# A hybrid encoder layer on one core: the low half of a split weight on VectorE or GpSimd

## The chip, the core and the metric

The kernel runs on one core of a Trainium2 chip. The metric is the device time of one execution in microseconds. The core has TensorE (matmul, "PE" in the profile, its weight loads "PEld"), VectorE ("DVE"), ScalarE ("ACT"), GpSimd ("POOL") and SyncE ("SP", here only the issuer of DMAs). Each engine works through its own stream of instructions in the order in which the program was written, and waits for others at semaphores.

## What is computed

One encoder layer over 512 tokens of 1024 features in float32: two token mixers in parallel, merged by gates, then a SwiGLU channel mixer.

```python
proj = h @ w_in[l]
qa, ka, va, qb, kb, vb = jnp.split(proj, SPLITS, axis=-1)
...
o_a = windowed_gqa_sink(qa, ka, va, a_sink[l])
o_b = dilated_mixture(qb, kb, vb)
gates = jax.nn.sigmoid(h @ w_gate[l] + b_gate[l])
g_a, g_b = jnp.split(gates, N_BRANCH, axis=-1)
mixed = g_a * (o_a @ w_br_a[l]) + g_b * (o_b @ w_br_b[l])
y = mixed @ w_out[l]
h = layer_norm(DN_ALPHA * h + y, ln1_g[l], ln1_b[l])
f = (jax.nn.silu(h @ w_ff_gate[l]) * (h @ w_ff_up[l])) @ w_ff_down[l]
h = layer_norm(DN_ALPHA * h + f, ln2_g[l], ln2_b[l])
```

Mixer A is windowed attention with 16 query heads and 4 key heads and a sink; mixer B is three dilated windows of attention, combined by their softmax denominators.

## The kernel before

**Split operands.** A float32 operand `w` is turned into `hi`, the value rounded to the format that TensorE takes at full pace, and `lo = w - hi`. Every product is then three matmuls: `hi*hi`, `hi*lo`, `lo*hi` (lines 456 to 458 in the projections and branches, 650 to 652 in mixer B's values, 1077 to 1079 in the output projection and the end of the channel mixer, 1312 to 1314 and 1441 to 1443 in the channel mixer). The weights come from HBM packed as `wpack` in units of 128x1024; a half unit is a tile of 128x512. `half_unit` (line 359) loads a half unit into a tile of class `ws`, takes two tiles of class `whl` for `hi` and `lo`, and calls `split` (line 350): first a copy that makes `hi`, by ScalarE or VectorE (`copy`, line 333 for ScalarE and 335 for VectorE), then the subtraction that makes `lo`, line 354, by VectorE. `unit` calls it twice, `token_values` (mixer B's values) calls `split` itself. The very first weights (line 382), the input (line 430), the attention's own operands (lines 528, 544, 563, 683, 702), the branches' moving operands (`split_of`, line 998) and the channel mixer's weights (`parts`, line 1199, by ScalarE and VectorE) have code of their own. So 130 subtractions come from line 354: 122 for `w_in`, the gates, the branches and `w_out`, 8 for the last rows of `w_ff_down`.

**Stages,** by the time in the trace: start of the projections (to 20 us), projections with mixer A between them (20 to about 230), with mixer B (240 to 345), the two branches and the gates' products (345 to about 390), output projection and first layer norm (to 446), channel mixer (446 to 740), its last rows, second layer norm and store (740 to 780). Attention is laid between the dense matmuls: for a unit of mixer A (a group of heads and 128 queries) scores (lines 578 and 579), a maximum and mask on VectorE (726), the exponential on ScalarE (730), a scaling by either (666, 668), four transposes on TensorE (678), a split by ScalarE and VectorE (333, 683), the product with the values (743, 744). A unit of mixer B has the same parts (786 to 818, 678 and 693, 870 and 904) and in its middle an exchange of statistics between partitions, 32 small copies on GpSimd (lines 828 and 829).

**The order.** No order is written out for the engines. Each operation is handed to `op` with a list of engines that may do it and a cost for each; `Program.run` (line 171) then plays the program forward with these costs, and whenever an engine is free it takes the ready operation with the lowest `prio`, and emits it. A copy has two possible engines. VectorE passes over an operation with more than one engine as long as ScalarE is free or is about to be:

```python
if o.ready <= now and (best is None or o.prio < best.prio) and self.fits(o):
    if e == DVE and len(o.alts) > 1 and free[ACT] < now + BIAS:
        continue
    best = o
```

`prio` is the time on TensorE's plan at which the operation was written down, plus an offset: -130 (`LOOK`) for weights, so that they are made early, -100 for what empties PSUM, 0 for attention's inner steps, -20 for the splits of line 998. `fits` holds an operation back while there are no free tiles of its class: 16 tiles `whl` until the last attention unit has ended, 40 then.

**GpSimd before** does 16 DMAs of the rotary tables (line 435), 64 copies of the sink (724) and four pairs of memsets (767, 768) for the attention units, 128 copies of mixer B's exchange (828, 829), 80 DMAs that add a second matrix to a weight tile on its way (1266), and four additions in the second layer norm (1129), ahead of which it is set up once for such arithmetic.

Of the kernel before, what the change touches and what calls it, by code (L numbers as in the profile page):

```python
# [13 lines left out]
ALU = mybir.AluOpType  # L14

P = 128
S = 512
# [28 lines left out]
PE, ACT, DVE, POOL, SP = "PE", "ACT", "DVE", "POOL", "SP"  # L46
# [6 lines left out]
N_BEGIN = 2  # L53
N_HALF = 3
N_LAST1, N_LAST, BY_POOL = 5, 4, (1, 2)
BANKS = dict(dense=3, s=2, tb=2, o=1, d=8)
UNITS = 2
D_BANK = "s"
# [39 lines left out]
class Program:  # L98
# [16 lines left out]
    def op(self, alts, fn, reads=(), writes=(), prio=0.0, after=(), abs_prio=None, moves=0.0):  # L115
        o = Op()
        o.urgent = self.urgent
        o.alts, o.fn = alts, fn
        o.prio = (self.T + prio if abs_prio is None else abs_prio, len(self.ops))
        o.ready, o.done, o.eng = 0.0, None, None  # L120
        deps = set(a for a in after if a is not None)
        for t in reads:
            deps.update(self.writer.get(t, ()))
        for t in writes:
            deps.update(self.writer.get(t, ()))
            deps.update(self.readers.get(t, ()))
        deps.discard(o)
        for t in reads:
            self.readers.setdefault(t, []).append(o)
        for t in writes:  # L130
            self.writer[t] = [o]
            self.readers[t] = []
        o.bufs, o.new = [], []
        o.strict, o.moves = self.strict, moves
        for t in list(reads) + list(writes):
            b = self.buf_of(t)
            if b not in o.bufs:
                o.bufs.append(b)
                b.users += 1
        o.succ = []  # L140
        o.left = len(deps)
        for d in deps:
            d.succ.append(o)
        self.ops.append(o)
        return o
# [134 lines left out]
def dve(n, fast=False, extra=0.0):  # L280
    return 0.069 + (0.00074 if fast else 0.00104) * n + extra
# [7 lines left out]
def hybrid_layer(ctx: ExitStack, tc: tile.TileContext, wpack, xT, xtok, sink, bgate,  # L289
                 ln1g, ln1b, ln2g, ln2b, ropec, ropes, maska, maskb, identd, out):  # L290
    nc = tc.nc
# [5 lines left out]
    N_SLOT = 85 - 2 * N_TWO  # L297
    pr = Program({"slot": N_SLOT, "bank": 8, **BANKS,
                  "ws": N_WS, "whl": N_WHL, "att": N_ATT, "gen": N_SLOT - 2 - N_ATT - N_WS - N_WHL,
                  "unit": UNITS, "st": 4, "x4": 4, "wf": N_WF, "two": N_TWO})  # L300
    op = pr.op
# [29 lines left out]
    def copy(eng, dst, src):  # L331
        if eng == ACT:
            nc.scalar.activation(dst, src, AF.Copy)  # L333
        else:
            nc.vector.tensor_copy(dst, src)

    def f32(ap):
        return ap.bitcast(F32)
# [5 lines left out]
    def cp_alts(n, ps=False):  # L344
        return [(ACT, act(n, ps)), (DVE, dve(n, not ps))]
# [4 lines left out]
    def split(src, h, l, prio=0.0, abs_prio=None, hold=()):  # L350

        op(cp_alts(S), lambda e: copy(e, h.t, src.t), reads=[src], writes=[h, *hold], prio=prio,
           abs_prio=abs_prio)
        op([(DVE, dve(S))], lambda e: nc.vector.tensor_tensor(l.t, src.t, f32(h.t), op=ALU.subtract),  # L354
           reads=[src, h], writes=[l], prio=prio, abs_prio=abs_prio)

    LOOK, LOOK_E, LOOK_W, LOOK_U, LOOK_T = 130.0, 80.0, 30.0, 15.0, (-300.0, -118.0, -114.5, -108.0)

    def half_unit(u, j, look=LOOK):
        st, h, l = slot(F32, "ws"), slot(F32R, "whl"), slot(F32R, "whl")  # L360
        load(st, wpack[u, :, j * S:(j + 1) * S], prio=-look)
        split(st, h, l, prio=-look, hold=[(l, "room")])
        return h, l
# [69 lines left out]
    for t_, src, ap in ((cosT, ropec, -119.5), (sinT, ropes, -119.4)):  # L433
        for i in range(8):
            op([(POOL, 1.0)], lambda e, t_=t_, i=i, src=src: nc.gpsimd.dma_start(t_.t[16 * i:16 * i + 16], src[0:16]),
               writes=[(t_, i)], abs_prio=ap, moves=0.1)
# [5 lines left out]
       reads=[nsink], writes=[nsink], abs_prio=-119)  # L442
# [189 lines left out]
    def token_values():  # L632

        parts_ = []
        for k in range(KD):
            st, h, l = slot(F32, "ws"), slot(F32R, "whl"), slot(F32R, "whl")
            u, c = U_VB + k // 4, (k % 4) * 256
            load(st, wpack[u:u + 3:2, :, c:c + 256].rearrange("g p c -> p g c"),
                 dst=lambda st=st: st.t.rearrange("p (g c) -> p g c", g=2), prio=-LOOK)
            split(st, h, l, prio=-LOOK, hold=[(l, "room")])  # L640
            parts_.append((h, l))
        res = ([], [])
        for r in range(NR):
            ps = bank("dense")
            for k in range(KD):
                wh, wl = parts_[k]

                def go(e, ps=ps, k=k, wh=wh, wl=wl, r=r):
                    a, b = xh[k]()[:, r * P:(r + 1) * P], xl[k]()[:, r * P:(r + 1) * P]
                    mm(ps.t, a, wh.t, start=(k == 0), stop=False)  # L650
                    mm(ps.t, a, wl.t, start=False, stop=False)
                    mm(ps.t, b, wh.t, start=False, stop=(k == KD - 1))

                op([(PE, 3 * pe(S))], go, reads=[wh, wl, *xtok_of(k)], writes=[ps])
                pr.T += 3 * pe(S)
            for g in range(2):
                res[g].append(value_split(ps, 256 * g))
        return res
# [350 lines left out]
    for f in range(16):  # L1009
        op([(ACT, act(S))], lambda e, f=f: nc.scalar.activation(gz[f].t, gz[f].t, AF.Sigmoid),  # L1010
           reads=[gz[f]], writes=[gz[f]], after=exps)
# [588 lines left out]
```

## Time and profile before

| | us |
|---|---|
| median of three runs | 781.47 (781.02 to 781.51) |
| the profiled execution's own time | 781.53 |
| its span, first to last instruction | 779.8 |
| ScalarE's copies, line 333, from SBUF and from PSUM, busy | 242.5 and 88.6 |
| line 354 on VectorE, busy | 87.0 |
| the exchange on GpSimd, lines 828 and 829, busy | 16.7 and 16.8 |

The page is one execution. Its groups read: line, engine, operation, output from inputs (`sl` a tile of the slab, `ps` a PSUM bank, `tw`, `x` other tiles, `st` statistics), count, busy time and mean of one, then how long the engine was idle before them and for whom. Stage rows read: the stretch, its length, then busy time and count of PE, PEld, DVE, ACT and POOL, the granted clock of TensorE, the DMA engines' share and GB/s. A timeline row is start, length, engine, line and operation. Work outside the span takes 781.53 - 779.8 = 1.7 us.

### The profile page before, as it was taken

How to read it: one execution, taken by the hardware profiler on the slowest of the kernel's cores; microseconds unless marked ns; L12 is line 12 of the kernel's file. 1: busy time of each engine (PE TensorE's matmuls, PEld its weight loads, DVE VectorE, ACT ScalarE, POOL GpSimd, SP SyncE). 2: the span in 40 equal slices, each digit the busy share in tenths (PEclk: the TensorE clock that was granted, in tenths of full speed). 3: DMA queues.
4: the chain of work that ended last, by engine and by line, in shares of the span. 5: the costliest groups of instructions: out<-in, count | busy, mean ns of one | idle time of the engine just before them, and what ended most of it. 6: DMA issues, size and time to landing. Idle time of an engine off the chain costs nothing.

```text
span 779.8 us, 13408 instructions
## 1 busy us (share of the span) xinstructions
PE 769.9 (99%) x4486; PEld 676.6 (87%) x4486; DVE 652.5 (84%) x1377; ACT 480.9 (62%) x1061; POOL 131.5 (17%) x304
## 2 busy tenths in 40 slices
PE   9999999999999999999999999999999999999996
PEld 5888888888888888888888899999999999999985
DVE  5689889898778999797687999887988889888697
ACT  5557787868757668794341667566655566555631
POOL 4100001100000801600011010242102331123002
PEclk9999999999999999999999999999999999999999
DMA  8642323213132324436373388689867987689102
GB/s 268 217 138 71 99 88 105 83 44 108 57 96 88 104 87 145 142 111 201 121 217 67 109 231 225 155 183 213 227 179 161 241 179 208 182 213 210 52 1 108
DMA packets 64901, 111.79 MB, mean 143 GB/s; under 512 B 8640, under 2 KB 12352, under 8 KB 64832
## 3 DMA queue, kind: packets, MB, share of 16 engines
q1 hardware_dynamic: 52656, 89.37, 35.5%
q0 software_dynamic: 12032, 21.50, 16.5%
q8 instruction: 35, 0.57, 0.3%
q14 instruction: 34, 0.28, 0.1%
q10 hardware_dynamic: 144, 0.07, 0.0%
HBM read 104.09 MB, written 3.93 MB: 139 GB/s over the span
## 4 chain that ended last, share of the span: by engine, by line
PE 93%; DVE 2%; ACT 1%; DMA 1%; issue 1%; SPq 1%; DVEq 0%
PE ps L457 11%; PE ps L456 11%; PE ps L458 11%; PE ps L1314 9%; PE ps L1313 9%; PE ps L1312 9%; PE ps L1441 4%; PE ps L1442 4%; PE ps L1443 4%; PE ps L1077 3%; PE ps L1079 3%; PE ps L1078 3%; PE ps L678 2%; PE ps L579 1%; PE ps L578 1%; PE ps L743 1%
## 5 line engine op out<-in xcount | busy, mean ns | idle before, releaser
L333 ACT ACTIVATE sl<-sl 128x512 fp32r<-128x512 f32 (+5 forms) x446 | 242.5, 571 | 65.9 <-DMA sl<-wpack 16.6
L1196 DVE TENSOR_TENSOR sl<-sl,sl 128x512 fp32r<-128x512 f32 (+3 forms) x304 | 169.9, 604 | 12.1 <-ACT sl L333 7.6
L333 ACT ACTIVATE sl<-ps 128x256 f32<-128x256 f32 (+4 forms) x206 | 88.6, 451 | 114.5 <-PE ps L1314 66.6
L456 PE MATMUL ps<-x,sl 128*128 128x512 f32 x336 | 133.7, 398 | 0.4 <-ACT sl L333 0.3
L457 PE MATMUL ps<-x,sl 128*128 128x512 f32 x336 | 131.9, 393 | 0.2 <-DVE x L430 0.2
L458 PE MATMUL ps<-x,sl 128*128 128x512 f32 x336 | 131.6, 392 | 0.0
L354 DVE TENSOR_TENSOR sl<-sl,sl 128x512 fp32r<-128x512 f32 x130 | 87.0, 687 | 9.3 <-ACT sl L333 6.5
L1266 POOL DMA_DIRECT2D sl<-wpack x44 | 39.8, 970 | 260.1 <-DMA sl<-wpack 111.6
L458 PEld LDWEIGHTS ps<-x,sl 128*128 128x128 f32 x336 | 63.1, 188 | 14.4 <-DVE sl L382 0.7
L1312 PE MATMUL ps<-x,sl 128*128 128x256 f32 x264 | 74.8, 283 | 0.0
L1314 PE MATMUL ps<-x,sl 128*128 128x256 f32 x264 | 74.7, 283 | 0.0
L1313 PE MATMUL ps<-x,sl 128*128 128x256 f32 x264 | 74.7, 283 | 0.0
L456 PEld LDWEIGHTS ps<-x,sl 128*128 128x128 f32 x336 | 63.2, 188 | 12.2 <-ACT x L333 1.0
L457 PEld LDWEIGHTS ps<-x,sl 128*128 128x128 f32 x336 | 63.3, 188 | 12.0 <-DVE x L430 1.8
L1196 DVE TENSOR_TENSOR sl<-sl,ps 128x512 f32<-128x512 f32 (+1 forms) x78 | 47.4, 611 | 25.7 <-PE ps L1314 16.6
L1312 PEld LDWEIGHTS ps<-x,sl 128*128 128x128 f32 x264 | 50.6, 192 | 0.5
L1313 PEld LDWEIGHTS ps<-x,sl 128*128 128x128 f32 x264 | 50.6, 192 | 0.5
L1314 PEld LDWEIGHTS ps<-x,sl 128*128 128x128 f32 x264 | 50.6, 192 | 0.0
L1314 PE MATMUL ps<-tw,sl 128*128 128x256 f32 x176 | 49.8, 283 | 0.0
L1313 PE MATMUL ps<-tw,sl 128*128 128x256 f32 x176 | 49.8, 283 | 0.0
L1314 PE MATMUL ps<-sl,sl 128*128 128x256 f32 x176 | 49.8, 283 | 0.0
L1313 PE MATMUL ps<-sl,sl 128*128 128x256 f32 x176 | 49.8, 283 | 0.0
(149 smaller groups left out, 1808.7 us busy)
## 6 DMA issues: line engine op xcount, KB each, us to landing
sl<-wpack SPq DMA_DIRECT2D x243, 256.0 KB, 3.4
sl<-wpack POOLq DMA_DIRECT2D x44, 256.0 KB, 5.2
wf<-wpack SPq DMA_DIRECT2D x36, 256.0 KB, 4.2
wf<-wpack POOLq DMA_DIRECT2D x36, 256.0 KB, 6.5
sl<-sl SPq DMA_DIRECT2D x88, 32.0 KB, 1.9
sl<-xT SPq DMA_DIRECT2D x8, 256.0 KB, 5.8
sl<-xtok SPq DMA_DIRECT2D x8, 256.0 KB, 2.7
gz<-sl SPq DMA_DIRECT2D x7, 256.0 KB, 2.2
```

Of the source, the lines that this page charges most:

```text
L333: nc.scalar.activation(dst, src, AF.Copy)
L354: op([(DVE, dve(S))], lambda e: nc.vector.tensor_tensor(l.t, src.t, f32(h.t), op=ALU.subtract), reads=[src, h], writes=[l], prio=prio, abs ...
L456: mm(o, a, x0, start=(k == 0), stop=False)
L457: mm(o, a, x1, start=False, stop=False)
L458: mm(o, b, x0, start=False, stop=(k == nk - 1))
L1196: op([(DVE, dve(w))], lambda e: nc.vector.tensor_tensor(dst(), x(), y(), op=o), reads=reads, writes=writes, prio=prio)
L1266: return op([(POOL, 1.0)], lambda e: nc.gpsimd.dma_start(dst.t, wpack[u, :, j * S:(j + 1) * S], accum_op=ALU.add), reads=[dst], writes=[ds ...
L1312: mm(o, wh, bh[k](), start=(first and k == 0), stop=False, skip_group_check=True)
L1313: mm(o, wh, bl[k](), start=False, stop=False, skip_group_check=True)
L1314: mm(o, wl, bh[k](), start=False, stop=(k == 3), skip_group_check=True)
L1441: mm(ps.t, x0, w[0].t, start=(first and m == 0), stop=False, skip_group_check=True)
L1442: mm(ps.t, x0, w[1].t, start=False, stop=False, skip_group_check=True)
```

## The change

The subtraction of `split` may be done by VectorE or by GpSimd. Its cost on GpSimd is written as 1.3.

```diff
+POOL_TT = 1.3
...
-        op([(DVE, dve(S))], lambda e: nc.vector.tensor_tensor(l.t, src.t, f32(h.t), op=ALU.subtract),
-           reads=[src, h], writes=[l], prio=prio, abs_prio=abs_prio)
+        op([(DVE, dve(S)), (POOL, POOL_TT)], lambda e: (nc.vector if e == DVE else nc.gpsimd).tensor_tensor(
+            l.t, src.t, f32(h.t), op=ALU.subtract), reads=[src, h], writes=[l], prio=prio, abs_prio=abs_prio)
```

The two files differ by one line ahead of the function, so line 354 of before is 355 of the change, and so on. Since the operation now has two engines, VectorE passes over it while ScalarE is free; GpSimd has no such rule. Of the 130 subtractions 96 come to stand on GpSimd: 90 ahead of the channel mixer and 6 of the 8 in the last rows. VectorE's stream goes from 1352 to 1280 rows: 96 subtractions less, and 24 copies more that ScalarE had. The setting up of GpSimd stands right behind its first 16 DMAs. The order of all engines is planned anew; TensorE's 4444 rows are the same instructions, 370 of them at another place. SyncE has the same 384 rows, 14 of them at another place.

On GpSimd, mixer A's first units (`sl` from `nsink` is the copy of the sink for one head of a unit). Before:

```order
L724 COPY sl_597<-nsink 128x1
L724 COPY sl_599<-nsink 128x1
L724 COPY sl_602<-nsink 128x1
L724 COPY sl_607<-nsink 128x1
L724 COPY sl_792<-nsink 128x1
```

With the change, the same place of the program:

```order
L725 COPY sl_596<-nsink 128x1
L355 TENSOR_TENSOR sl_582<-sl_433,sl_581 128x512
L725 COPY sl_636<-nsink 128x1
L725 COPY sl_638<-nsink 128x1
L725 COPY sl_644<-nsink 128x1
L725 COPY sl_647<-nsink 128x1
L355 TENSOR_TENSOR sl_632<-sl_459,sl_631 128x512
L355 TENSOR_TENSOR sl_756<-sl_508,sl_755 128x512
L725 COPY sl_780<-nsink 128x1
```

Splits of weights now stand ahead of and between the units' copies. In mixer B the same holds for the exchange: two splits stand ahead of the last 8 of the first unit's 32 copies, and one ahead of the last 8 of the last unit's.

On VectorE, the end of the last attention unit and the start of the branches (L998 makes a branch's moving operand, L913 ends the attention unit, L908 is the step ahead of it). Before:

```order
L998 TENSOR_TENSOR sl_4226<-tw_2243,sl_4225 128x512
L354 TENSOR_TENSOR sl_4252<-sl_3892,sl_4251 128x512
L908 TENSOR_TENSOR sl_4239<-sl_4239,ps_4177 128x512
L998 TENSOR_TENSOR sl_4229<-tw_2243,sl_4228 128x512
L998 TENSOR_TENSOR sl_4244<-sl_3513,sl_4243 128x512
L913 TENSOR_TENSOR sl_4112<-sl_4239,sl_4276 64x512
L335 CAST sl_4288<-sl_3929 128x512
L335 CAST sl_4303<-sl_4040 128x512
L354 TENSOR_TENSOR sl_4289<-sl_3929,sl_4288 128x512
L354 TENSOR_TENSOR sl_4294<-sl_3978,sl_4293 128x512
```

With the change:

```order
L909 TENSOR_TENSOR sl_4176<-sl_4176,ps_4123 128x512
L336 COPY sl_4212<-sl_4176 64x512
L914 TENSOR_TENSOR sl_4068<-sl_4176,sl_4212 64x512
L336 CAST sl_4229<-tw_1774 128x512
L999 TENSOR_TENSOR sl_4221<-tw_1332,sl_4220 128x512
L336 CAST sl_4254<-sl_4066 128x512
L336 CAST sl_4261<-sl_4163 128x512
L999 TENSOR_TENSOR sl_4227<-tw_1774,sl_4226 128x512
L355 TENSOR_TENSOR sl_4255<-sl_4066,sl_4254 128x512
L355 TENSOR_TENSOR sl_4259<-sl_4110,sl_4258 128x512
L355 TENSOR_TENSOR sl_4262<-sl_4163,sl_4261 128x512
L999 TENSOR_TENSOR sl_4230<-tw_1774,sl_4229 128x512
```

The attention unit now ends before most of the branches' operands are made, and copies and splits of both kinds stand mixed, while GpSimd has splits of its own beside them.

## The prediction, before the changed kernel was run

> **What bounds the kernel now.** I read the page's table of engines and its chain first, then the busy times by stage, then single matmuls.
>
> ```profile
> span 779.8 us, 13408 instructions
> PE 769.9 (99%) x4486; PEld 676.6 (87%) x4486; DVE 652.5 (84%) x1377; ACT 480.9 (62%) x1061; POOL 131.5 (17%) x304
> PE 93%; DVE 2%; ACT 1%; DMA 1%; issue 1%; SPq 1%; DVEq 0%
> ...
> 60.00:240.00 180.00, 180.00 (x923) 152.91 (x922) 152.41 (x369) 133.37 (x312) 11.04 (x56) 1.00 0.27 85
> 240.00:345.00 105.00, 104.81 (x543) 88.29 (x543) 92.73 (x250) 80.06 (x194) 33.03 (x131) 1.00 0.35 111
> 345.00:360.00 15.00, 15.00 (x68) 12.43 (x67) 13.57 (x24) 13.06 (x25) 0.00 (x0) 1.00 0.63 204
> ```
>
> TensorE carries 93% of the chain, and in the three stages that make the moved instructions (mixer A, mixer B, start of the branches) it is busy 180.00 of 180, 104.81 of 105 and 15.00 of 15 us. A busy row can hide a wait, since a matmul's record is longer than its turn, so the next rows are starts.
>
> ```profile
> 299.98 0.39 PE L457 MATMUL ps<-x,sl 128*128 128x512 f32 x1
> 300.21 0.39 PE L458 MATMUL ps<-x,sl 128*128 128x512 f32 x1
> ...
> 60.38 1.03 PE L678 MATMUL ps<-ident,sl 128*128 128x128 f32 x8
> 78.91 0.60 PE L678 MATMUL ps<-ident,sl 128*128 128x128 f32 x4
> 289.10 1.37 PE L678 MATMUL ps<-ident,sl 128*128 128x128 f32 x8
> 289.70 0.53 PEld L678 LDWEIGHTS ps<-ident,sl 128*128 128x128 f32 x5 [0.35 <-DVE sl L668]
> 334.22 0.95 PE L678 MATMUL ps<-ident,sl 128*128 128x128 f32 x4
> ```
>
> A 512-column matmul starts 0.23 us after the one before it at a clock of 1.00: TensorE is at its own pace. Real waits inside the affected stages are few. Eight transposes take 1.03 us undisturbed and 1.37 at 289.10 (VectorE's normalisation came 0.35 late); four take 0.60, and 0.95 at 334.22. Both ends of mixer-B units together lose 0.34 + 0.35 = 0.69 us. That is about **all that a less loaded VectorE can give back**. VectorE is 85% to 90% busy there and off the bound.
>
> **What the change does, and its price.** By the order of both programs, 96 of the 130 subtractions leave VectorE for GpSimd, and 24 copies that ScalarE made before are now VectorE's; TensorE has the same instructions, some in another order.
>
> ```profile
> L354 DVE TENSOR_TENSOR sl<-sl,sl 128x512 fp32r<-128x512 f32 x130 | 87.0, 687 | 9.3 <-ACT sl L333 6.5 <-issue 0.9 <-ACT sl L927 0.5
> L1129 POOL TENSOR_TENSOR sl<-sl,sl 128x512 f32<-128x512 f32 x4 | 5.1, 1284 | 35.7 <-ACT sl L1127 35.7
> L335 DVE CAST sl<-sl 128x512 fp32r<-128x512 f32 x16 | 6.7, 425 | 0.1
> ```
>
> VectorE loses 96 x 0.687 = 66.0 us and takes 24 copies of some 0.4 us (estimate from the 425 ns row; others are shorter and longer), about 10: net 56 us less. GpSimd gains 96 x 1.284 = 123.3 us, priced by its own addition of the same tile size. None of this is on TensorE.
>
> *Are the weights late?* One split gives half a unit, on which TensorE works 12 matmuls x 0.227 = 2.7 us, so one GpSimd at 1.28 keeps up. The cover (VectorE's record, and TensorE's first use of the same tile) at the start, in the middle, and in the last stage:
>
> ```profile
> 20.35 0.69 DVE L354 TENSOR_TENSOR sl<-sl,sl 128x512 fp32r<-128x512 f32 x1 [1.43 <-ACT sl L333]
> 24.08 0.39 PE L458 MATMUL ps<-x,sl 128*128 128x512 f32 x1
> ...
> 251.19 0.69 DVE L354 TENSOR_TENSOR sl<-sl,sl 128x512 fp32r<-128x512 f32 x1
> 270.85 0.39 PE L458 MATMUL ps<-x,sl 128*128 128x512 f32 x1
> ...
> 742.75 1.89 DVE L354 TENSOR_TENSOR sl<-sl,sl 128x512 fp32r<-128x512 f32 x3
> 746.10 0.39 PE L1078 MATMUL ps<-sl,sl 128*128 128x512 f32 x1
> ```
>
> At first 24.08 - 21.04 = 3.0 us, in the middle 19, in the last stage 746.10 - 743.44 = 2.7. Each is more than the 0.6 us by which GpSimd is slower, so I price lateness at **zero**. In the last stage six of the eight splits stand in a row on GpSimd: 742.75 + 6 x 1.284 = 750.5, while the last two are first used at 754; bound there 1 us if GpSimd is held up.
>
> *What does VectorE pay for GpSimd's reads?* No row of before has the two engines reading long tiles from SBUF at once. The nearest rows are GpSimd's tiny copies of statistics:
>
> ```profile
> 253.64 0.67 DVE L354 TENSOR_TENSOR sl<-sl,sl 128x512 fp32r<-128x512 f32 x1
> ...
> 253.70 0.66 POOL L828 COPY st<-st 32x2 f32<-32x2 f32 x1
> 254.40 0.18 POOL L829 COPY st<-st 32x2 f32<-32x2 f32 x1
> ```
>
> Alone such a copy takes 0.18 us. The one that starts 0.06 us behind a subtraction of two SBUF tiles ends at 254.36, 0.05 us after that subtraction. GpSimd is held for the whole VectorE instruction. Whether VectorE is held the same way by a GpSimd instruction isn't shown, since 0.18 us is too short to see. So one meeting costs VectorE from 0 to 1.284 us. I take the symmetric reading, a wait for what is left of the GpSimd instruction, 0.64 us on average, because the row of the one direction is a full hold.
>
> The Trainium skill, "SBUF — State Buffer", section "Who interferes with whom", speaks against this change: a VectorE instruction with two SBUF inputs, or in a two-port mode, and a GpSimd instruction that reads SBUF share one port pair, and whichever comes second is blocked until the other ends. The trace agrees in the direction it can show (0.66 for 0.18 us). By that rule the price is the one I take; without it the sum below would have only the gain.
>
> How often do they meet? What VectorE keeps of this kind (two SBUF inputs, or a copy or scaling from SBUF in the fast form):
>
> ```profile
> L528 DVE TENSOR_TENSOR sl<-sl,sl 64x512 fp32r<-64x512 f32 x28 | 19.3, 688 | 1.0
> L668 DVE TENSOR_SCALAR sl<-sl,st 128x256 f32<-128x256 f32 x25 | 7.9, 350 | 0.3
> L668 DVE TENSOR_SCALAR sl<-sl,st 128x384 f32<-128x384 f32 x14 | 5.4, 418 | 0.2
> L998 DVE TENSOR_TENSOR sl<-sl,sl 128x512 fp32r<-128x512 f32 x14 | 9.6, 688 | 2.9 <-ACT sl L333 2.9
> L998 DVE TENSOR_TENSOR sl<-tw,sl 128x512 fp32r<-128x512 f32 x8 | 5.2, 683 | 0.0
> ```
>
> With the 16 casts above and 32 splits that stay on VectorE before 415 us, these are 28 + 25 + 14 + 14 + 8 + 16 + 32 = 137 (smaller groups left out). Ninety of the moved splits fall between 20 and 415 us: GpSimd is in one for 90 x 1.284 = 116 of 395 us, 29%. So some 0.29 x 137 = 40 meetings, 40 x 0.64 = 26 us of waits on VectorE, against 56 us that it gains. VectorE is still better off in sum; the price is **where** the waits fall.
>
> ```profile
> 29.27 0.69 DVE L335 COPY sl<-ps 128x512 f32<-128x512 f32 x1 [0.44 <-PE ps L458]
> 30.43 0.60 PE L611 MATMUL ps<-ident,sl 128*128 128x128 f32 x4
> ...
> 358.11 0.68 DVE L998 TENSOR_TENSOR sl<-sl,sl 128x512 fp32r<-128x512 f32 x1
> 359.47 0.39 PE L457 MATMUL ps<-sl,sl 128*128 128x512 f32 x1
> ```
>
> Matching the trace to the program's order gives, for each matmul, the end of the instruction that made its operand. Between 20 and 420 us there are 55 products of VectorE or ScalarE that TensorE starts on within 0.9 us of their end; those above are the first and the last (0.5 and 0.7 us), and the mean is 0.60. Behind each lies about 2 us of VectorE and ScalarE work (a copy and a subtraction of 0.6 to 0.7 each, and their hand-overs). A meeting falls into such a stretch with 40/395 x 2 = 20%; of waits spread evenly from 0 to 1.284 us, 53% exceed 0.60, by 0.34 on average. TensorE waits 55 x 0.20 x 0.53 x 0.34 = **2.0 us**; with no cover at all 55 x 0.20 x 0.64 = 7.0; with no hold 0.
>
> *GpSimd's own queue.* It also makes mixer B's exchange of statistics, 32 copies a unit, on which the normalisation waits. In the changed order two splits stand inside the first unit's copies and one inside the last unit's. Each puts its unit's end 1.284 us later. The planner has moved other matmuls in, but two unit ends already had no cover (0.34 and 0.35 us above). From 0 to 3 x 1.284 = 3.9 us; I take **1.0**, nearer to zero, since only one of the three is in a unit that TensorE waited for.
>
> Sum against the profiled execution's 781.53 us (span 779.8, and 1.7 around it; the median of three is 781.47, the same within 0.06): 781.53 - 0.7 + 0 + 2.0 + 1.0 = **783.8 us**, 0.3% slower.
>
> **Rivals.**
> *VectorE is not held* (or only until GpSimd's next element), and the exchange is covered: 781.53 - 0.7 = 780.8, up to 783.0 where the cover takes most of the waits. For it: 26 us of waits against 56 us freed, and splits made 19 us ahead. Against it: the full hold at 253.70.
>
> *Faster by more than 1.6 us.* It would need waits that I don't see: the two unit ends give 0.7, and the rest runs at 0.23 us a matmul. 779.5; only a better interleaving on TensorE could bring it.
>
> *GpSimd's code arrives late.*
>
> ```profile
> 9.00 0.96 POOL L435 DMA_DIRECT2D sl<-ropes x2 [0.56 <-DMA sl<-ropec]
> ...
> L1129 POOLq MODIFY_POOL_CONFIG  x2: 354/354/354, 732.0 to 732.0; - x2
> 765.75 1.29 POOL L1129 TENSOR_TENSOR sl<-sl,sl 128x512 f32<-128x512 f32 x1 [33.47 <-ACT sl L1127]
> ```
>
> GpSimd is set up for its tile arithmetic once, in before 33.4 us ahead of the first use. Now this stands behind the DMAs that end at 9.96, 10.4 us ahead of the first split. If what follows it takes more than 24.08 - 1.28 - 9.96 = 12.8 us, TensorE waits at 24 us, at most 33.4 - 12.8 = 20.6 us: 781.5 to 802. The Trainium skill, "GPSIMD Engine Reference", section "2.1 Instruction dispatch", has about 6 us for a first call, which would be hidden; no run here shows it.
>
> That the change doesn't do what it says is out: 96 splits stand on GpSimd.
>
> **How the numbers follow.** About 0.2% (1.6 us) is what a measurement of this kernel can tell from no change. Forecast, held VectorE and a later exchange, 783.0 to 789: 0.52. Not held or covered, 780.7 to 783.0: 0.40. Faster, below 779.9: 0.05. Late code: 0.03. So faster 0.05, same 0.40, slower 0.55. The likeliest time is 783.8. The range starts at the whole relief without a price (780.7) and goes to 789.0, that is the 7.0 us with no cover and a little of the exchange; the full 3.9 and 7.0 together (792) and late code are left out. The forecast's own range is 783.0 to 789.0.
>
> **What would show it.** Right: GpSimd's subtractions beside VectorE's two-input ones, with VectorE's mean at L998, L528 or L668 well above 687, 688 and 350 ns; more and longer gaps before the transposes and value products of the attention units and at the first branches near 340 us; TensorE's pace in 446 to 740 us unchanged. Wrong: VectorE's means unchanged and TensorE's waits gone (the rival), the gaps only at 289 and 334 us (the exchange), or a hole at 24 us (late code). A lone late stretch at 742 to 755 us would mean that the last stage's cover of 2.7 us was too thin, which I price at zero.

## The result, and the profile after

The changed kernel takes 804.54 us (median of five runs, 803.28 to 805.82) where the kernel before takes 781.47. The ratio is 1.0297, with a 95% interval of 1.0282 to 1.0312. That is 23.1 us slower, where 2.3 were forecast.

First the head of the page of the changed kernel: the span and the busy time of each engine. One caution before it is used: line N of the kernel before is line N + 1 here.

```profile
span 802.8 us, 13452 instructions
PE 779.2 (97%) x4486; PEld 679.5 (85%) x4486; DVE 648.9 (81%) x1306; ACT 467.7 (58%) x1036; POOL 258.8 (32%) x400
```

VectorE has lost 96 subtractions and taken 28 copies, for 3 scalings that went to ScalarE, yet its busy time fell by only 652.5 - 648.9 = 3.6 us, where the prediction had 56 freed. The first experiment below, which leaves GpSimd's reads out, shows that 652.5 - 611.1 = 41.4 us were freed and 37.8 came back as longer instructions. The groups by line and shape show which (count, then busy us and mean ns, then the idle time ahead):

```profile
L355 POOL TENSOR_TENSOR sl<-sl,sl 128x512 fp32r<-128x512 f32 x96 | 133.4, 1398 | 240.0 <-ACT sl L334 167.5
L355 DVE TENSOR_TENSOR sl<-sl,sl 128x512 fp32r<-128x512 f32 x34 | 30.4, 908 | 6.2 <-ACT sl L334 4.8 <-POOL sl L769 1.0
L529 DVE TENSOR_TENSOR sl<-sl,sl 64x512 fp32r<-64x512 f32 x28 | 24.6, 878 | 3.7 <-ACT sl L334 2.3 <-issue 0.5
L999 DVE TENSOR_TENSOR sl<-tw,sl 128x512 fp32r<-128x512 f32 x8 | 8.6, 1090 | 0.0
L336 DVE CAST sl<-sl 128x512 fp32r<-128x512 f32 x22 | 14.3, 656 | 0.1
L669 DVE TENSOR_SCALAR sl<-sl,st 128x256 f32<-128x256 f32 x23 | 9.1, 422 | 0.2
L684 DVE TENSOR_TENSOR sl<-ps,sl 128x512 fp32r<-128x512 f32 x48 | 31.7, 685 | 6.2 <-ACT sl L334 4.1 <-POOL sl L725 1.9
```

The two-input subtractions went from 688 to 878 ns and from 683 to 1090, the cast from 425 to 656, the scaling from 350 to 422. L684, which reads one input from PSUM, stays at 685. GpSimd pays too: 1398 ns for a split, not 1284.

Next TensorE, by stage (stretch, length, busy time and count of PE, PEld, DVE, ACT and POOL, then the granted clock):

```profile
60.00:240.00 180.00, 175.42 (x876) 146.81 (x875) 143.91 (x326) 121.81 (x284) 58.32 (x96) 0.99 0.25 79
240.00:345.00 105.00, 102.62 (x521) 86.02 (x520) 87.25 (x232) 71.03 (x180) 57.12 (x153) 0.98 0.33 103
345.00:360.00 15.00, 12.51 (x66) 10.29 (x65) 13.30 (x22) 13.59 (x28) 7.31 (x6) 0.98 0.60 192
360.00:420.00 60.00, 59.58 (x256) 48.60 (x256) 40.73 (x54) 21.97 (x39) 26.27 (x20) 0.98 0.50 157
446.00:740.00 294.00, 293.89 (x2127) 278.18 (x2126) 258.67 (x484) 177.04 (x378) 63.74 (x73) 1.00 0.79 194
```

The stretches are times of this run; the work in them has slid by up to 18 us against the kernel before (the table further down). The channel mixer in the middle keeps its pace. In the first three rows TensorE is now idle for 4.6, 2.4 and 2.5 us, where it was idle for 0, 0.2 and 0, and in the first four rows the mean clock is 0.98 or 0.99, where it was 1.00. The largest waits behind the idle time (TensorE's line and the line waited for: us, times, longest):

```profile
PE ps L679 <- ACT sl L667: 2.6, 3, 1.9
PE ps L579 <- DVE sl L529: 2.1, 3, 1.6
PE ps L458 <- DVE sl L999: 2.0, 1, 2.0
PE ps L1442 <- DVE sl L1197: 1.9, 2, 1.1
PE ps L679 <- DVE sl L669: 1.8, 1, 1.8
```

One of them from close by, in the timeline (start, length, engine, line; PE, then VectorE, then GpSimd) at the start of the branches:

```profile
356.45 0.39 PE L457 MATMUL ps<-sl,sl 128*128 128x512 f32 x1
358.86 0.50 PE L458 MATMUL ps<-sl,sl 128*128 128x512 f32 x1 [2.03 <-DVE sl L999]
359.20 0.39 PE L459 MATMUL ps<-sl,sl 128*128 128x512 f32 x1
...
355.66 1.47 DVE L336 CAST sl<-tw 128x512 fp32r<-128x512 f32 x1
357.06 1.75 DVE L999 TENSOR_TENSOR sl<-tw,sl 128x512 fp32r<-128x512 f32 x1
...
355.56 2.70 POOL L355 TENSOR_TENSOR sl<-sl,sl 128x512 fp32r<-128x512 f32 x2 [0.93 <-ACT sl L334]
```

GpSimd makes two splits in a row. VectorE's cast starts 0.10 us behind the first and takes 1.47 us for 0.43; its subtraction meets the second and takes 1.75 for 0.68. The two engines take turns, and the lo for which TensorE's next matmul waits is late. The matmul at 358.86 starts 2.41 us behind the one before it, and not 0.23.

Last, how late TensorE is in all. The table gives the start of the matmul with the same count (of 4486) less its start in the kernel before, in us; the columns to the right belong to the experiments below.

| at (us, before) | the change | writes alone | plan on VectorE | hold counted | hold counted, writes alone | only behind |
|---|---|---|---|---|---|---|
| 95 | 2.6 | 0.2 | 0.8 | -0.1 | 0.5 | 0.2 |
| 147 | 7.3 | 0.9 | 3.6 | 1.7 | 1.9 | 0.3 |
| 240 | 8.8 | 0.9 | 4.8 | 0.6 | 0.9 | 0.5 |
| 283 | 12.7 | 0.4 | 6.3 | 0.6 | 0.9 | 0.8 |
| 330 | 12.3 | 0.0 | 7.2 | 1.7 | 2.0 | 0.8 |
| 345 | 17.1 | 1.2 | 9.1 | 6.2 | 6.5 | 1.7 |
| 740 | 18.4 | 1.2 | 10.5 | 6.2 | 6.5 | 1.7 |
| 756 | 23.0 | 1.2 | 12.3 | 7.2 | 6.5 | 5.0 |

### The profile page after: what moved, and what is told of

Read it like the earlier page. It is cut to its first block, busy times and chain, and to the rows that moved or that the text cites. A ratio compares the mean times of both kernels' runs of the same rounds, so it can differ in the third digit from the quotient of the medians.

```text
span 802.8 us, 13452 instructions
## 1 busy us (share of the span) xinstructions
PE 779.2 (97%) x4486; PEld 679.5 (85%) x4486; DVE 648.9 (81%) x1306; ACT 467.7 (58%) x1036; POOL 258.8 (32%) x400
## 5 line engine op out<-in xcount | busy, mean ns | idle before, releaser
L334 ACT ACTIVATE sl<-sl 128x512 fp32r<-128x512 f32 (+4 forms) x433 | 234.9, 570 | 97.0 <-PE ps L458 27.0
L355 POOL TENSOR_TENSOR sl<-sl,sl 128x512 fp32r<-128x512 f32 x96 | 133.4, 1398 | 240.0 <-ACT sl L334 167.5
L1197 DVE TENSOR_TENSOR sl<-sl,sl 128x512 fp32r<-128x512 f32 (+3 forms) x304 | 169.7, 603 | 8.7 <-ACT sl L334 7.5
L334 ACT ACTIVATE sl<-ps 128x256 f32<-128x256 f32 (+4 forms) x193 | 81.2, 441 | 104.7 <-PE ps L1315 67.2
L1197 DVE TENSOR_TENSOR sl<-sl,ps 128x512 f32<-128x512 f32 (+1 forms) x78 | 47.4, 610 | 25.2 <-PE ps L1315 16.7
L1267 POOL DMA_DIRECT2D wf<-wpack x36 | 35.4, 1186 | 75.9 <-DVE sl L1197 60.8
L1442 PE MATMUL ps<-sl,sl 128*128 128x512 f32 x126 | 49.6, 394 | 1.9 <-DVE sl L1197 1.9
L1444 PE MATMUL ps<-sl,sl 128*128 128x512 f32 x126 | 49.1, 390 | 1.0 <-DVE sl L1197 1.0
L1443 PE MATMUL ps<-sl,sl 128*128 128x512 f32 x126 | 49.5, 393 | 0.5 <-DVE sl L1197 0.5
```

The source lines that it names most:

```text
L355: op([(DVE, dve(S)), (POOL, POOL_TT)], lambda e: (nc.vector if e == DVE else nc.gpsimd).tensor_tensor(l.t, src.t, f32(h.t), op=ALU.subtrac ...
L1197: op([(DVE, dve(w))], lambda e: nc.vector.tensor_tensor(dst(), x(), y(), op=o), reads=reads, writes=writes, prio=prio)
L1267: return op([(POOL, 1.0)], lambda e: nc.gpsimd.dma_start(dst.t, wpack[u, :, j * S:(j + 1) * S], accum_op=ALU.add), reads=[dst], writes=[ds ...
L1442: mm(ps.t, x0, w[0].t, start=(first and m == 0), stop=False, skip_group_check=True)
L1443: mm(ps.t, x0, w[1].t, start=False, stop=False, skip_group_check=True)
```

## The experiments

Theory 1: GpSimd's reads of SBUF hold up VectorE's instructions, VectorE falls behind, and TensorE waits. Rival 2: the new order, with GpSimd's small copies queued behind the splits. Rival 3: each lo comes later because GpSimd takes longer for it. Each run stands against runs of the kernel before on the same chip (781.3 to 781.6 us).

### Writes alone

The edit, shortened:

```
-  (nc.vector if e == DVE else nc.gpsimd).tensor_tensor(l.t, src.t, f32(h.t), op=ALU.subtract)
+  if e == DVE: nc.vector.tensor_tensor(l.t, src.t, f32(h.t), op=ALU.subtract)
+  else:
+      nc.gpsimd.tensor_copy(l.t[:, :1], f32(h.t[:, :1]))
+      for _ in range(2): nc.gpsimd.memset(f32(l.t), 0.0)
```

> The change's plan, order and engines are kept, but where GpSimd made a lo it now writes zeros over the tile twice and reads only one column of hi (the lo of these 96 half units is left out, so their third products add nothing). Theory 1 (GpSimd's reads of SBUF hold up VectorE's instructions, and that reaches TensorE): VectorE's 128x512 cast of L336 falls from 656 back to about 425 ns and the half-block difference of L999 from 1090 to about 683, and the time falls to 781 to 785 us. Rival 2 (the new order, and GpSimd's own copies queued behind the splits): the queue and the order are as in the change, so it stays at 801 to 805 us. Rival 3 (the lo weights come later because GpSimd takes 1.4 us for one): also 801 to 805, as long as two writes and a copy last about as long as a split.

Measured: 782.89 us, ratio 1.0020 (1.0010 to 1.0029). The engines and groups of this run:

```profile
PE 770.2 (99%) x4486; PEld 677.0 (87%) x4486; DVE 611.1 (78%) x1306; ACT 468.5 (60%) x1036; POOL 250.5 (32%) x592
L362 POOL MEMSET sl<- 128x512 f32 x192 | 103.7, 540 | 11.2
L360 POOL CAST sl<-sl 128x1 fp32r<-128x1 f32 x96 | 25.9, 270 | 219.4 <-ACT sl L334 187.2 <-DVE sl L336 27.1 <-PE ps L466 1.5
L1007 DVE TENSOR_TENSOR sl<-tw,sl 128x512 fp32r<-128x512 f32 x8 | 5.3, 680 | 0.0
L336 DVE CAST sl<-sl 128x512 fp32r<-128x512 f32 x22 | 9.9, 458 | 0.1
```

GpSimd is occupied as long (2 x 540 + 270 = 1350 ns, a split took 1398), in the same order, and its results are as late. Without its reads VectorE has 648.9 - 611.1 = 37.8 us less to do, with the same instructions in the same order, and 804.54 - 782.89 = 21.6 us of the 23.1 are gone. Rivals 2 and 3 and the relief of VectorE together leave 1.4 us. Theory 1 holds.

### Half the reading

The lo of the same 96 half units becomes one copy and one setting to zero: `nc.gpsimd.tensor_copy(l.t, f32(h.t))`, then `nc.gpsimd.memset(f32(l.t), 0.0)`.

> The change's plan, order and engines, but GpSimd's share of a half unit is a copy of hi over the lo tile (one input read from SBUF) and then zeros over it (the lo of these 96 is left out, their third products add nothing). If any GpSimd instruction that reads SBUF holds VectorE for its length: VectorE's busy time stands between the run with writes alone (611 us) and the change (649 us), in the share of the copy's length in a split's 1.3 us, some 620 to 640 us, and the time is 786 to 799 us. If only an instruction with two inputs holds it: VectorE stays at 611 us and the time at 782 to 784.5 us.

Measured: 785.44 us, ratio 1.0051 (1.0034 to 1.0068), VectorE busy 620.5 us.

```profile
L360 POOL CAST sl<-sl 128x512 fp32r<-128x512 f32 x96 | 66.9, 697 | 235.9 <-ACT sl L334 199.5 <-DVE sl L336 32.9 <-issue 3.3
L1006 DVE TENSOR_TENSOR sl<-tw,sl 128x512 fp32r<-128x512 f32 x8 | 6.1, 785 | 0.0
```

One input is enough to hold VectorE, so the first branch of the expectation is right in kind; the time fell 0.6 us below its range. The copy lasts half as long as a split, but VectorE is held for 620.5 - 611.1 = 9.4 us, a quarter of 37.8, and TensorE pays 2.6 us over the writes alone, an eighth of 21.6. The price rises faster than the hold.

### The same order, with the splits back on VectorE

Only the engine of the instruction is changed, behind the plan: `lambda e: nc.vector.tensor_tensor(...)` for either choice.

> The change's plan and order, but every lo that the plan gave to GpSimd is issued on VectorE at the same place of the program (130 on VectorE, none on GpSimd). Theory 1 (reads of GpSimd hold VectorE): no GpSimd read, so durations as before the change; VectorE has its 66 us of splits back at places where the plan had thought it free, so 781.5 to 786 us. Rival 2 (the order): most of the 23 us stays, 795 to 805 us. Rival 3 (lateness from 1.4 us a split): the splits take 0.69 us again, 781.5 to 786.

Measured: 794.26 us, ratio 1.0164 (1.0149 to 1.0179). Theory 1 expected up to 786, so this was a miss. The order itself costs little (the run of writes alone has the same one). What this run shares with the change is **time of VectorE that the plan does not know of**: 664.1 - 611.1 = 53 us, which cost 11.4 us. The table shows the loss in the same places as the change's, some half as large.

### Reads beside the old order

The edit, shortened:

```
+  also = this split is one of the 96
   nc.vector.tensor_tensor(l.t, src.t, f32(h.t), op=ALU.subtract)
+  if also:
+      for c in (0, S // 2):
+          nc.gpsimd.tensor_tensor(warm.bitcast(F32), f32(h.t[:, :S // 2]), f32(h.t[:, S // 2:]), op=ALU.subtract)
```

> The kernel before, with its order on every engine, VectorE making all 130 lo; beside 96 of them (the same half units that the change gives to GpSimd) GpSimd also subtracts the two halves of hi from one another, twice, into a scratch tile that nobody reads. Nobody waits for GpSimd's result, so no weight comes later but for what VectorE loses. Theory 1: VectorE's two-input and cast instructions lengthen as in the change, and VectorE has 66 us more to do than there: 795 to 812 us. Rivals 2 and 3 without the hold: only the copies and exchanges behind these reads in GpSimd's queue could be late, 781.5 to 786 us.

Measured: 820.89 us, ratio 1.0504 (1.0487 to 1.0522), above even theory 1's range. VectorE's busy time is 702.8 us, 50.3 more than before. Nothing of the old order was touched and nobody waits for these results: reads of GpSimd do it by themselves. (GpSimd's own small copies stand behind these reads too, which this run doesn't separate; with writes alone such a queue was part of only 1.4 us.)

### The last stage

The half units of the last products stay on VectorE: `op([(DVE, dve(S)), (POOL, POOL_TT)][:1 + by_pool], ...)` with `by_pool=u < U_DOWN`.

> The change with only the half units of the last products (eight splits, of which the change gives six to GpSimd) kept on VectorE. All else is the change. The lag of TensorE's rows grows by 4.6 us between 756 and 773 us in the change; theory 1 puts all of it down to VectorE's sums of L1197 held by these six splits: 799.5 to 800.5 us. Rival 2 (the order of the last stage was changed by what came before): 803 to 805.

Measured: 800.16 us, ratio 1.0240 (1.0224 to 1.0255): 4.4 us less than the change. The timeline of the change shows how the six splits did it (PE, VectorE, GpSimd):

```profile
764.09 0.39 PE L1444 MATMUL ps<-sl,sl 128*128 128x512 f32 x1
765.53 0.47 PE L1442 MATMUL ps<-sl,sl 128*128 128x512 f32 x1 [1.05 <-DVE sl L1197]
...
763.01 1.78 DVE L355 TENSOR_TENSOR sl<-sl,sl 128x512 fp32r<-128x512 f32 x1
764.71 0.68 DVE L1197 TENSOR_TENSOR sl<-sl,ps 128x512 f32<-128x512 f32 x1
765.31 1.16 DVE L1197 TENSOR_TENSOR sl<-wf,sl 128x512 fp32r<-128x512 f32 x1
766.39 1.77 DVE L355 TENSOR_TENSOR sl<-sl,sl 128x512 fp32r<-128x512 f32 x1
...
762.88 8.11 POOL L355 TENSOR_TENSOR sl<-sl,sl 128x512 fp32r<-128x512 f32 x5 [0.41 <-PE ps L1444]
```

Five splits run back to back, and every instruction of VectorE with two SBUF inputs waits for one of them, while the one with a PSUM input passes in 0.68. What comes late is not the lo that GpSimd makes: it is the weights of the channel mixer's last products, made by VectorE in L1197.

### A few splits only

```
+  if e == POOL and len(o.alts) > 1 and free[DVE] < now + 0.6:
+      continue
```

> The change, but the planner gives a lo to GpSimd only where VectorE still has over 0.6 us of work before it when GpSimd could begin: 26 lo instead of 96. Theory 1: each lo on GpSimd costs as the mean of the change does, 21.6 us by 96, so 26 cost about 6 us, less what the stalls of 2 us and their clock took: 783 to 789 us. A rival (only the few holds at the ends of stages cost, and these are also where VectorE is behind): 795 or more. If taking work off VectorE where it is behind were worth something: below 781.

Measured: 786.48 us, ratio 1.0063 (1.0048 to 1.0078), as expected. By the table 3.3 of the 5.0 us arise in the last stage, where five of the 26 splits run in a row on GpSimd (8.12 us from 744.89 on).

### A plan that counts the hold

The edit of the planner, shortened:

```
+  start = now
+  if e == POOL and len(o.alts) > 1:
+      start = max(now, port[DVE]); port[POOL] = start + cost
+  elif e == DVE and not any("bank" in b.keys for b in o.bufs):
+      start = max(now, port[POOL]); port[DVE] = start + cost
-  end = now + cost
+  end = start + cost
```

> The change, with the planner told of the hold: a lo made by GpSimd and an instruction of VectorE that touches no PSUM bank start, in the plan alone, one after the other. The computation and its instructions are those of the change, 96 lo still go to GpSimd, and only order and engine choices move. Theory 1a (the holds hurt because VectorE falls behind a plan that does not count them, so that the wrong thing stands first in its queue): most of the 21.6 us between the change and the run with writes alone comes back, 783 to 791 us, and TensorE waits for VectorE less than 4 us in all. Theory 1b (the holds hurt in themselves, a late instruction of VectorE is late whatever the plan says): 796 to 804 us.

Measured: 789.35 us, ratio 1.0102 (1.0085 to 1.0119): 15.2 us less than the change and within the range of theory 1a. GpSimd has no fewer splits, 100 by the trace and not the 96 of the expectation. To see what of the rest is the hold, the same plan ran with writes alone (again 100, where the expectation says 96):

> The plan that counts the hold, with its order and engines (96 lo on GpSimd, 789.35 us with real splits), but GpSimd writes zeros over the lo tile twice and reads one column of hi, as in the run with writes alone (these 96 lo are left out). If what is left over before (7.7 us, 4.5 of them between 330 and 345 us) is made by the holds themselves: 781.5 to 784 us, and the rows at 345 us stand within 1.5 us of before. If it is made by the order that this plan gives (ScalarE's copies at the last heads of mixer B): 786 to 790 us, with the late stretch at 335 to 342 us still there.

Measured: 788.10 us, ratio 1.0079 (1.0062 to 1.0096), in the second of its ranges. The engines of the two runs, first with splits, then with writes:

```profile
PE 772.9 (98%) x4486; PEld 678.5 (86%) x4486; DVE 633.2 (80%) x1268; ACT 484.7 (62%) x1070; POOL 267.4 (34%) x404
...
PE 772.4 (98%) x4486; PEld 678.8 (86%) x4486; DVE 593.9 (76%) x1268; ACT 484.5 (62%) x1070; POOL 255.0 (32%) x604
```

The hold is as large as ever, 633.2 - 593.9 = 39.3 us (37.8 in the change), but in this order it costs 789.35 - 788.10 = 1.2 us, which the intervals hardly tell from nothing. In the change's order it cost 21.6. So the price of a hold was made by **the plan it fell into**, and not by its length alone. That this plan absorbs the hold because it counts it is the natural reading. It isn't shown by itself: the plan also gave 34 instructions more to ScalarE, so that without reads VectorE has 611.1 - 593.9 = 17.2 us less to do than in the change, and a plan that absorbs the hold by chance is not excluded.

What is left of this plan, 6.6 us without any reads, belongs to its order: 4.5 of them, by the table, between 330 and 345 us. There a table load of 1.28 us and sigmoids of ScalarE stand ahead of the last heads' scalings. They do in the kernel before too, but 3.5 us earlier: the load is at 330.23 there and at 333.72 here. A stretch at half clock (see the section on the clock) begins at 342.1 and is part of the 4.5. Three runs went after it. One kept all half units from the branches on on VectorE, one in addition used GpSimd only where VectorE was planned busy for 0.3 us more, and one let the sigmoids begin only after the last scaling (`after=exps + norms`).

> The change with the planner told of the hold, and the half units of the branches, w_out and the last products kept on VectorE: 67 lo go to GpSimd, all for the two mixers and the gates. Theory 1a: TensorE's rows ran only 0.6 to 1.0 us late at the end of the mixers when the plan counted the holds, and nothing is moved behind that: 781.5 to 784 us. Theory 1b (each hold costs in itself, wherever it is): 67 of 96 at 0.08 us, 786 to 788 us.

> As the run before, and GpSimd takes a lo only where the plan has VectorE busy for another 0.3 us: 46 lo. If taking work off VectorE is worth something once holds are planned and the last stages are left alone, this is the version that would show it: 779 to 781 us. Theory 1a, with the run of writes alone, says that there is nothing to gain, since TensorE waits for VectorE under 1 us in all in the kernel before: 781 to 783.5 us.

> The plan that counts the hold (96 lo on GpSimd, all computed), and the 16 sigmoids of the gates may begin only when all scalings of probabilities are issued in the plan, so that their table load of 1.28 us and the first sigmoids no longer stand ahead of the last heads' scalings on ScalarE; ScalarE's order before them is the same. If the 4.5 us that this plan loses between 330 and 345 us come from the sigmoids: 783.5 to 786 us, and TensorE's rows at 345 us are 1.5 to 2.5 us behind the kernel before. If they come from holds of GpSimd or elsewhere in the order: 788 to 790 us.

The first two missed: ratios 1.0082 (1.0067 to 1.0097; 787.68 us) and 1.0103 (1.0086 to 1.0120; 788.35 to 790.33 us). The first fell into the range of theory 1b, that each hold costs in itself; but the run with writes alone puts the holds of the whole plan at 1.2 us, so another reason is likelier. It is 1.1 us late at 283 us, as expected, and 7.1 at 345, though its GpSimd does nothing at all between 330 and 350 us of its own time: the loss there isn't made by holds of splits in that stretch. The third gave 787.20 us, ratio 1.0075 (1.0060 to 1.0091), between its two ranges and so a miss too (98 splits on GpSimd). In its profiled execution the clock stays at 1.00 there, and its rows lose 2.7 us instead of 4.5 between 330 and 345. That difference is about what the stretch at half clock takes (1.7 us), so what the later sigmoids bring by themselves isn't shown. What makes the rest of this plan's order slower is left open.

Last, the third run with the last stage's splits on VectorE, the best that these pieces give:

> The run before with the lo of the last products kept on VectorE (91 on GpSimd): every place known to cost is taken out. If VectorE's relief were worth something once nothing is late: below 781 us. If there is nothing to gain, as the run of writes alone says: 782 to 784.5 us, level with that run.

Measured: 785.92 us, ratio 1.0059 (1.0042 to 1.0075), above both of its ranges: not every place that costs was known. No version beat the kernel before, and the run of writes alone, in which VectorE had 41 us less to do than before, didn't either.

### The clock

The changed kernel has three stretches at half clock, behind waits of 1.85, 1.86 and 2.03 us; a wait of 1.6 us at 94.8 had none behind it. In these stretches 512-column matmuls start 0.43 us apart (three windows, the granted clock is the number behind the last count, and three matmuls):

```profile
142.00:144.00 2.00, 2.00 (x8) 1.71 (x8) 1.83 (x5) 1.83 (x6) 0.53 (x1) 0.50 0.00 0
284.00:286.00 2.00, 2.00 (x9) 1.65 (x8) 0.96 (x4) 2.00 (x6) 1.47 (x7) 0.61 0.15 36
360.00:362.00 2.00, 2.00 (x6) 1.54 (x6) 2.00 (x3) 2.00 (x5) 0.82 (x2) 0.50 0.00 0
...
285.33 0.63 PE L457 MATMUL ps<-x,sl 128*128 128x512 f32 x1
285.76 0.63 PE L458 MATMUL ps<-x,sl 128*128 128x512 f32 x1
286.19 0.63 PE L459 MATMUL ps<-x,sl 128*128 128x512 f32 x1
```

To measure it by itself, the kernel before got one wait in the middle of the channel mixer:

```
+  mm(o, warm[:, :P], warm[:, :HP], start=False, stop=False, skip_group_check=True)
+  for _ in range(N): nc.vector.memset(warm, 0.0)
+  mm(o, warm[:, :P], warm[:, :HP], start=False, stop=False, skip_group_check=True)
```

> The kernel before, and in the middle of the channel mixer (its pace of 294 us had no wait) TensorE is made to wait once: a matmul by zeros, five settings to zero by VectorE of 0.27 us each that wait for it, and another matmul by zeros that waits for them. Nothing is left out. The wait should be 1.4 to 1.8 us long. If only waits of about 2 us or more are followed by a stretch at half clock: no slice below full clock, and 1.6 to 2.2 us over before. If any wait does it: 1.7 us more, 3.3 to 3.9 us over.

> The same with ten settings to zero: a wait of 2.8 to 3.2 us. If waits of 2 us or more are followed by 3.4 us at half clock, as in the profile of the change: a stretch with starts 427 ns apart and 1.7 us beside the wait, 4.6 to 5.1 us over before. If the half clock in the change's profile had another cause: 2.9 to 3.4 us over before and no such stretch.

The two waits, and the clock behind the longer one:

```profile
PE ps L1319 <- DVE warm L1318: 2.0, 1, 2.0
...
PE ps L1319 <- DVE warm L1318: 4.0, 1, 4.0
...
572.00:573.00 1.00, 0.25 (x3) 0.26 (x4) 0.85 (x4) 0.00 (x0) 0.00 (x0) 1.00 0.00 0
573.00:574.00 1.00, 1.00 (x9) 1.00 (x8) 1.00 (x2) 0.19 (x1) 0.00 (x0) 0.79 0.06 16
574.00:575.00 1.00, 1.00 (x6) 1.00 (x6) 1.00 (x3) 0.71 (x2) 0.00 (x0) 0.50 0.00 0
576.00:577.00 1.00, 1.00 (x7) 1.00 (x7) 0.56 (x1) 0.00 (x0) 0.00 (x0) 0.51 0.77 277
577.00:578.00 1.00, 1.00 (x10) 1.00 (x10) 0.73 (x2) 0.83 (x2) 0.00 (x0) 1.00 0.22 82
```

Both waits were longer than meant, so the ranges expected, for shorter ones, don't hold as they stand. The one of 4.0 us cost 787.69 - 781.63 = 6.1 us: TensorE's next product starts 572.79 - 568.49 = 4.3 us late, and 1.7 us are what 3.4 us at half clock take away. The one of 2.0 us cost 3.2 us in the median and gave two kinds of runs: 783.44 and 784.03 us at a mean clock of 0.997, and 784.79, 785.16 and 785.68 at 0.995. The difference of their means is 1.5 us, near the 1.7 of one stretch. So a wait of about 2.0 us seems to bring the half clock in some executions and not in others; the one execution with a profile, of 783.44 us, had none.

## Why the prediction was wrong in size

*VectorE held by GpSimd's reads, and by how much.* Right in kind, and too small in amount: 26 us of waits were forecast, 37.8 measured. VectorE's instructions are the same in the change and with writes alone, so they can be compared one by one. Ahead of the channel mixer 45 of them are over 0.1 us longer in the change, by 36.4 us in all: 40 meetings of 0.64 us were forecast, and 45 of 0.81 came. The kinds of instructions were right too.

*What of it reaches TensorE.* This step failed: 55 x 0.20 x 0.53 x 0.34 = 2.0 us, with 7.0 as the bound, for 21.6 measured (17.2 of it ahead of the last stage, by the table: 18.4 - 1.2 at 740). It took the meetings one by one: a product is late only if a meeting falls into the last 2 us of its making, and only by what its own cover of 0.60 us leaves. What it left out is that each instruction behind a held one in VectorE's queue starts later than in the plan that set the order, and that on an engine planned 85% to 90% busy one wait need not be made good before the next comes. So the bound was no bound: it counted only waits in the last 2 us, and not what was already late. The runs bear this out without following single waits: 53 us of VectorE's time that the plan didn't know of cost 11.4 us with no hold at all, 9.4 us of hold cost 2.6, 37.8 cost 21.6, and 39.3 in a plan that counts them 1.2. I had even written that VectorE is better off in sum and the price is where the waits fall; I then priced it as if they fell at random on a queue with slack.

*The clock.* Not considered. Three stretches of 3.4 us at half speed take 3 x 1.7 = 5.1 us from TensorE in the profiled execution, so at most that much of the 21.6.

*Lateness of the lo, zero.* Right for the lo itself: with writes alone, as late as the splits, the time is 1.4 us over. But the last stage was examined only for the six lo (bound 1 us), and it cost 4.4, by the waits of TensorE in it through the weights that VectorE makes beside them. The sign named for that case, a lone late stretch there, did appear, with another cause.

*Relief -0.7, and GpSimd's queue +1.0.* With lateness they are what the writes alone show, +1.4 us (0.8 to 2.3 by the interval), for +0.3 forecast. The net 56 us that VectorE was to gain were 41.4 with writes alone. The 66 us for 96 splits were sums of records, and a record runs into the next (in the kernel before seven splits in a row take 4.30 us at 348.86, 0.61 each); the 28 copies, many from PSUM at 0.69 us, took more than the 10 set down. Since TensorE hardly waited for VectorE, this changed nothing in the sum. The queue's part went wrong: that run loses nothing in mixer B (0.9 us late at 240, 0.0 at 330) and its 1.2 us between 330 and 345.

*The rivals.* VectorE not held: out. Faster: out; a relief of 41 us in the writes alone brought nothing, as the reading of before had it, with TensorE waiting for 0.7 us. Late code: no hole at 24 us, the rows are 0.3 us early at 45.

## What to carry to other kernels

Work moved to an idle engine is not free when the two engines hold one another up: read the means of the *unmoved* instructions first, and add their lengthening to the busy time of the engine that was to be relieved. If a plan fixes the order, give it that cost before moving anything: here a hold of the same size cost 21.6 us in a plan that didn't count it and 1.2 in one that did, though that one also gave VectorE less to do and was still slower than the kernel before. And if the bound engine waits for the engine to be relieved for only 0.7 us in all, there is little to gain: 41 us of relief without reads brought nothing.

## What the runs showed of the hardware

GpSimd's writes alone leave a two-input subtraction at 680 ns but lengthen VectorE's casts from SBUF, from 425 to 458 ns at 128x512 (and at 64x256 from 289 to 383); with the splits back on VectorE and nothing on GpSimd these casts stand at 422 and 288. The Trainium skill, "SBUF — State Buffer", section "Who interferes with whom", has just this: two SBUF inputs contend with GpSimd's reads and not with its writes, and the two-port modes, which a cast can enter, contend with GpSimd altogether. The runs agree.

The clock fell behind waits of 1.85 to 2.03 us, and in the plan that counts the hold even behind several short ones (longest 0.6 us, TensorE busy 3.42 of 5 us):

```profile
335.00:340.00 5.00, 3.42 (x17) 2.05 (x16) 2.61 (x7) 4.94 (x11) 2.45 (x2) 1.00 0.00 0
340.00:345.00 5.00, 4.36 (x18) 3.50 (x18) 3.91 (x8) 5.00 (x13) 0.09 (x1) 0.71 0.14 50
```

The Trainium skill, "TensorE: Matmul & The Clock Gate", section "What's actually happening", names an idle window of some 3.4 us that runs free of the kernel. The stretches of 3.4 us at half clock and the two kinds of runs at one wait of 2.0 us agree with such a window; that waits of 1.85 to 2.03 us, well below its length, sufficed is what these runs add.

The traces show why the length of a wait alone doesn't decide. The three stretches of the changed kernel start at 141.07, 284.43 and 359.53 us, 42 and 22 times 3.413 us apart, and TensorE was busy for 37%, 45% and 41% of the 3.413 us ahead of them. With the same grid laid over other runs, a wait of 3.3 us (reads beside the old order, at 292 us) lay across an edge and left TensorE busy for 51% and 53% of two slices, and the profiled wait of 2.0 us left 75% and 66%; behind neither did the clock fall. The plan that counts the hold doesn't fit: there it fell behind slices of 66% and 69%. So this is no full rule.
